# A hybrid decoder layer on one core: in blocks two to four the first two in-projection units multiply slice by slice, in two other PSUM banks

## The chip, the cores and the metric

The kernel runs on one core of a Trainium2 chip. The core has five engines that work side by side, each with its own instruction list, and they wait for one another through semaphores: TensorE (PE in the profile; its weight loads, PEld, overlap its matmuls), VectorE (DVE), ScalarE (ACT), GpSimd (POOL) and SyncE (SP), which here does nothing but issue DMA transfers. An engine takes its list strictly in order: an instruction that waits holds up everything behind it on that engine.

The metric is the device time of one execution in microseconds. Lower is better.

## The reference, cut to what matters

One layer over 2048 tokens of width 1024, in float32:

```python
h = rmsnorm(x, norm_mix_w) * (1 + sc1) + sh1
proj = h @ w_in                                   # 1024 x 3624
(hq, hf, hi, hg, sq, sk, sv, iq, ik, iw, cu) = split(proj)
o_a = hgrn2_mixer(hq, hf, hi, hg, ...)            # 4 heads, gated linear recurrence, chunkwise
o_b = dsa_mixer(sq, sk, sv, iq, ik, iw)           # indexer, top 256 keys per query, softmax
o_c = conv_module(cu, ...)                        # gate, causal depthwise conv (31 taps), LayerNorm, swish
x = x + g1 * (concat[o_a, o_b, o_c] @ w_out)
h = rmsnorm(x, norm_mlp_w) * (1 + sc2) + sh2
x = x + g2 * (relu(h @ W1) ** 2 @ W2)             # hidden width 4096
return rmsnorm(x, final_norm_w)
```

The part that matters here is `h @ w_in`, and the attention `dsa_mixer` and recurrence `hgrn2_mixer` that run beside it.

## The kernel before, in words

**Precision.** A float32 operand of a large matmul is split into a high and a low part (`ah`, `al` for activations; `whi`, `wlo`, or `wk` when both come back from a copy in HBM, for weights). One product is three matmuls: high by high, high weight by low activation, low weight by high activation.

**Blocks.** The 2048 tokens are done in four blocks of 512 (`b` is 0 to 3 in the code; the text says block one to four). For each block `in_block` does the norm, turns the activations, and then goes through 26 units of columns of `w_in` (`in_units`: 23 of 128 columns, and three of 256 that are done by L1280). A unit of 128 columns is 8 slices of 128 rows by three matmuls, so 24 matmuls of 128x512 into one PSUM bank (`mm_T`, L424). The first three units are the index keys with the index weights (`ev_index_k`) and the two index query units (`ev_iq`). The text calls them unit 0, unit 1 and unit 2; unit 3 is the first one of the recurrence.

**Turning the activations.** `to_act_steps` does one slice `k` of eight at a time: four PE transposes of 128x128 into a bank (L281), an ACT scale and shift into `tf` (L286), an ACT cast to the high part `ah` (L287) and the low part `al` by subtraction on DVE for slices 1, 4 and 6, on POOL for the others (L288). Every second slice the `mid` callback advances the recurrence of the block before.

**PSUM.** There are eight banks. The tag `mm` has two (transposes of slices and the units), `ax` two (the recurrence and small sums), `cx` one (convolution), `po` one (attention output) and `at` two. In this first half of the program the two `at` banks belong to the attention: its scores (L965), its turned probabilities (L987), the small turns L1011 and L1017, a count of the top-k search (L929) and the index scores (L808).

**Queues of side work.** After every unit a `step()` pumps generators: the recurrence (`fast`), the convolution, the modulation vectors, the index scores, the top-k search (DVE passes L917 with some small instructions, L918 to L926) and the attention (`at`). In blocks one to three, query tiles 0 to 5 of the attention are done; the others come later, beside the MLP. Per head the attention goes: scores on PE (L965), bias and maximum on DVE (L967, L976), exponential on ACT (L981), turn on PE (L987), copy and cast on ACT (L995, L996), low part on POOL (L997), product on PE (L999), and at the end of a head L1008 on ACT, L1009 on POOL, L1011 on PE, L1012 on ACT, L1013 on POOL.

**Who sets the order.** The program is recorded in the order of the code, and a scheduler then lays out each engine's list: it takes what it believes to be ready, earlier recorded work first, and gives a tile its bank only when the tile that had the bank before has been let go. So an instruction whose bank is still held is put behind others that were recorded later.

**Weights.** In blocks two to four the split weights of `w_in` come back from HBM (`wk<-wk_d`, issued on SP at L107) into slots used in turn: two units share the four `whi` and four `wlo` slots (of half a unit each), every third unit uses the two `wraw` slots. So unit 3 loads into the slots of unit 0, and can begin only when unit 0 has multiplied.

Of the kernel before, what the change touches and what calls it, by code (L numbers as in the profile page):

```python
# [43 lines left out]
KO, NPF = 2, 2  # L44
# [34 lines left out]
def trunk(ctx, tc, x, c, ada_w, ada_b, norm_mix_w, norm_mlp_w, w_in, hg_lb_logits,  # L79
# [22 lines left out]
    def nm(s):  # L102
        uid[0] += 1
        return f"{s}_{uid[0]}"
# [21 lines left out]
    def ps_at():  # L126
        return pp.tile([P, 512], F32, tag="at", bufs=2, name=nm("at"))

    def ps_xp(i):
        return {'0': ps_ax, '1': ps_mm, '2': ps_at, '3': ps_po}[XP[i]]()  # L130
# [79 lines left out]
    sh1 = cst.tile([P, NK], F32, name="sh1")  # L210
    a1 = cst.tile([P, NK], F32, name="a1")
# [63 lines left out]
    def to_act_steps(xh, acol, bcol, ah, al, mid=None):  # L275
        for k in range(NK):
            guard = tc.high_priority(offset=HA)
            guard.__enter__()
            pt = {'0': ps_ax, '1': ps_mm, '2': ps_at, '3': ps_po}[(TA2 if px['ax'] < 3 else TA)[k]]()
            for t in range(4):  # L280
                T.transpose(pt[:, t * P:(t + 1) * P], xh[t][:, k * P:(k + 1) * P], ident)  # L281
            hi = ap.tile([P, TB], F32R, tag="ah", bufs=8, name=nm("ah"))
            lo = ap.tile([P, TB], F32R, tag="al", bufs=8, name=nm("al"))
            tf = xp.tile([P, TB], F32, tag="tf", bufs=2, name=nm("tf"))
            ac, bc = acol[:, k:k + 1], bcol[:, k:k + 1]
            A.activation(tf, pt, AF.Identity, scale=ac, bias=bc)  # L286
            A.copy(hi, tf)  # L287
            (V if k in (1, 4, 6) else G).tensor_tensor(lo, tf, hi.bitcast(F32), OP.subtract)  # L288
            guard.__exit__(None, None, None)
            ah.append(hi)  # L290
            al.append(lo)
            if mid is not None and k % 2:
                mid()
            yield

    def to_act(xh, acol, bcol, mid=None):
        act = [], []
        for _ in to_act_steps(xh, acol, bcol, *act, mid):
            pass
        return act  # L300
# [22 lines left out]
    def by_k(tiles):  # L323
        return [t[:, k] for t in tiles for k in range(t.shape[1])]
# [73 lines left out]
    def next_w(pf=PF, ps=PS):  # L398
        top_up(pf, ps)
        w, sp = ready.pop(0)  # L400
        given.append((w, sp))
        return [by_k(t) for t in w]
# [12 lines left out]
    def mm_T(ps, w, act, k_outer=False, mid=None, k0=0, k1=NK):  # L415
        hi, lo = w
        ah, al = act
        prod = ((hi, ah), (hi, al), (lo, ah))
        if k_outer:
            order = [(k, p) for k in range(k0, k1) for p in prod]  # L420
        else:
            order = [(k, p) for p in prod for k in range(NK)]
        for n, (k, (ww, aa)) in enumerate(order):
            T.matmul(ps, ww[k], aa[k], start=(n == 0 and k0 == 0), stop=(n == len(order) - 1 and k1 == NK))  # L424
            if mid is not None and n == 11:
                mid()
# [603 lines left out]
    def pump(q, ns):  # L1030
        credit[q] += ns
        while queues[q] and credit[q] > 0:
            try:
                with tc.high_priority(offset=HF if q == "fast" else HC if q == "conv" else -LP):
                    r = next(queues[q][0])
                if r is None:
                    credit[q] = 0.0
                    break
                credit[q] -= r
            except StopIteration:  # L1040
                queues[q].pop(0)
        if not queues[q]:
            credit[q] = min(credit[q], 0.0)
# [21 lines left out]
    rates = {"fast": FAST, "conv": CR, "ada": 300.0, "idx": R1[0], "tk": R1[1], "at": R1[2]}  # L1065
# [30 lines left out]

    early = []

    def first_units(xts):
        act = [], []  # L1100
        steps = to_act_steps(xts, a1, sh1, *act)
        ws = []
        for k in range(NK // 2):
            next(steps)
        for u in range(KO):
            ws.append(next_w())
            early.append(ps_at())
            mm_T(early[u], ws[u], act, True, None, 0, NK // 2)
        ada_half(1, TB, a1, "nmix", far)
        ada_half(0, TB, sh1, None, far2)  # L1110
        for _ in steps:
            pass
        for u in range(KO):
            mm_T(early[u], ws[u], act, True, None, NK // 2, NK)
        return act

    def in_block(b, xts, nxt):
        act = first_units(xts) if b == 0 else to_act(xts, a1, sh1, lambda: pump("fast", rates["fast"]))
        for u, (pieces, ev, m) in enumerate(in_units):
            if ev is ev_cb:  # L1120
                drain("conv")
            if ev is ev_hf:
                drain("fast", 1)
            if u == PREP and b == NB - 1:
                yield "prep"
            if u == 1 and b == 0:
                late_consts()
            if b == 0 and u < len(early):
                ps = early[u]
            elif ev in (ev_hi, ev_sv):  # L1130
                ps = []
                halves = [[a[kh * 4:(kh + 1) * 4] for a in act] for kh in range(2)]
                ws = [next_w()]
                for tp_ in range(2):
                    ps.append(ps_xp(14 + tp_))
                    for kh in range(2):
                        if len(ws) < 2 and kh:
                            ws.append(next_w(1, 0))
                        n_part(ps[tp_], tp_, halves[kh], ws[kh], kh == 0, kh == 1)
                        if tp_ and kh:  # L1140
                            top_up()
                        half()
                    if tp_ == 0:
                        ev(b, m, ps[0], 0)
                        yield
            else:
                w = next_w()
                ps = ps_mm()
                mm_T(ps, w, act, u in (0, len(in_units) - 1), half)
            with tc.high_priority(offset=HE):  # L1150
                if ev is ev_index_k:
                    ev(b, ps)
                elif ev in (ev_hi, ev_sv):
                    ev(b, m, ps[1], 1)
                else:
                    ev(b, m, ps)
            keep_w()
            if ev is ev_ca and m == 1:
                queues["conv"].append(conv_gen(b))
            if ev is ev_hg:  # L1160
                queues["fast"].append(hgrn_gen(b, m, hg["q"], hg["k"], hg["f"], hg["v", m], hg["gate"]))
            yield
            if u == 2:
                yield "idx"
            if ev is ev_sv:
                yield "qkv"
            if u == NX:
                nxt()
# [498 lines left out]
```

## Time and profile before

| | |
|---|---|
| three runs, device us | 2903.92, 2909.93, 2911.09; median 2909.93 |
| the profiled execution | 2909.95, of which the span of the profile is 2908.2 |
| TensorE, busy and share of the span | 2781.8, 96% |
| VectorE | 1676.6, 58% |
| ScalarE | 1239.7, 43% |
| GpSimd | 1086.4, 37% |
| mean granted TensorE clock | 0.984 |
| the three stretches in which the activations of blocks two, three and four are turned (PE, from the first transpose to the first matmul of unit 0) | 243.9 to 261.3, 491.8 to 511.0, 741.4 to 755.1 |

A matmul's busy time in the profile includes a tail that overlaps the next one: thirteen of 128x512 in a row last 3.15 us, so they start 0.23 us apart, though each alone is shown with 0.39. For passes of 128x128 the figures are 0.27 shown and 0.11 apart. Sums of work below go by starts.

The idle time before an instruction is put down to what it waited for last. Engines other than TensorE are far from full over the whole span, but not everywhere: a stretch has to be looked at by itself.

### The profile page before, as it was taken

Reading aid. Unit: us, or ns where it says so; the run is one execution under the profiler, and the core shown is the slowest. Engines: PE = TensorE matmul, PEld = TensorE weight load, DVE = VectorE, ACT = ScalarE, POOL = GpSimd, SP = SyncE. Lnnn points to the kernel's source line nnn. Section 1 sums busy time; section 2 is a strip of 40 time slices with the busy share of each in tenths; the row PEclk is TensorE's granted clock in tenths of the full one; section 3 lists DMA queues with packets and bytes.
Section 4 is the critical chain, followed back from the end, with each engine's and each line's share of the span. In section 5 each row is a group of like instructions: output and inputs, shape, how many; then the busy total and the mean of one; then the engine's idle time right before and its main releaser. Section 6 shows DMA issues by size and latency. Waiting matters only on the chain.

```text
span 2908.2 us, 42801 instructions
## 1 busy us (share of the span) xinstructions
PE 2781.8 (96%) x14116; PEld 2306.0 (79%) x14116; DVE 1676.6 (58%) x3514; ACT 1239.7 (43%) x2630; POOL 1086.4 (37%) x1051
## 2 busy tenths in 40 slices
PE   5999998999999989999999999999999998999997
PEld 4888887888788777888777888887788887777776
DVE  6695697777465437656757637477662221254455
ACT  4436444533311244555556444354643332343323
POOL 7444111212100445666665222234422223345444
PEclk9999999999999989999999999999999999999999
DMA  9987676667655668898888776677867666686676
GB/s 292 291 268 243 215 234 190 218 209 245 202 183 180 221 218 255 272 291 284 292 266 295 231 221 216 202 243 258 289 211 237 200 226 197 217 284 209 224 235 206
DMA packets 428074, 688.61 MB, mean 237 GB/s; under 512 B 43383, under 2 KB 171452, under 8 KB 427836
## 3 DMA queue, kind: packets, MB, share of 16 engines
q1 hardware_dynamic: 427680, 685.67, 72.9%
q8 instruction: 113, 1.85, 0.3%
q14 instruction: 125, 1.02, 0.1%
q10 hardware_dynamic: 156, 0.07, 0.0%
HBM read 532.74 MB, written 152.84 MB: 236 GB/s over the span
## 4 chain that ended last, share of the span: by engine, by line
PE 41%; DMA 5%; DVE 4%; POOL 1%; issue 1%; ACT 0%; SPq 0%; POOLq 0%; DVEq 0%; ACTq 0%
PE mm L1304 10%; PE mm L424 9%; PE ax L424 7%; PE ax L1304 6%; PE mm L1464 4%; PE at L965 1%; PE po L999 1%; DMA wk<-wk_d 1%; PE at L987 1%; PE ix L808 1%; DMA tr<-in_mlp_w_dram 1%; PE at L1304 1%; DVE s L815 1%; DVE cum L917 1%; POOL wk L376 1%
## 5 line engine op out<-in xcount | busy, mean ns | idle before, releaser
L424 PE MATMUL mm<-ah,wk 128*128 128x512 f32 x1920 | 513.2, 399 | 4.1 <-DVE slo L537 1.7
L424 PEld LDWEIGHTS mm<-ah,wk 128*128 128x128 f32 x1920 | 355.7, 190 | 78.5 <-DVE slo L537 2.0
L318 POOL TENSOR_TENSOR wlo<-wraw,whi 128x512 fp32r<-128x512 f32 x210 | 285.8, 1380 | 245.2 <-ACT whi L317 133.6
L997 POOL TENSOR_TENSOR pT<-L,pT 128x512 fp32r<-128x512 f32 (+3 forms) x160 | 193.3, 1210 | 374.9 <-ACT pT L996 194.3
L815 DVE SCALAR_TENSOR_TENSOR s<-r,iw_s,s 128x512 f32<-128x512 f32 (+3 forms) x266 | 239.2, 899 | 104.2 <-ACT r L810 95.6
L424 PE MATMUL mm<-al,wk 128*128 128x512 f32 x960 | 262.4, 395 | 0.0
L967 DVE CUSTOM_DVE_ANT_0 L<-at,bias 128x512 f32<-128x512 f32 (+3 forms) x152 | 93.6, 619 | 206.0 <-PE at L965 156.7
L424 PEld LDWEIGHTS mm<-al,wk 128*128 128x128 f32 x960 | 178.3, 189 | 36.0
L1304 PE MATMUL mm<-wk,hh 128*128 128x512 f32 x640 | 197.8, 398 | 1.5 <-ACT tf L286 1.1
L810 ACT ACTIVATE r<-ix 128x512 f32<-128x512 f32 (+3 forms) x256 | 133.2, 554 | 151.6 <-PE ix L808 113.0
L317 ACT CAST whi<-wraw 128x512 fp32r<-128x512 f32 x210 | 122.1, 620 | 162.6 <-DMA wraw<-in_mlp_w_dram 47.9
L273 POOL TENSOR_TENSOR hl<-hr,hh 128x512 fp32r<-128x512 f32 x96 | 129.6, 1351 | 161.3 <-ACT hh L265 159.5
L424 PE MATMUL ax<-ah,wk 128*128 128x512 f32 x720 | 187.1, 393 | 1.4 <-DMA wk<-wk_d 1.4
L588 DVE SCALAR_TENSOR_TENSOR cx<-hc,cvc,cx 128x512 f32<-128x512 f32 x232 | 173.7, 749 | 2.0
L917 DVE TENSOR_SCALAR_CACHE_REDUCE cum<-s,ssm 128x384 bf16<-128x384 f32 (+13 forms) x112 | 165.3, 1476 | 7.3 <-POOL s L819 5.2
L995 ACT COPY L<-at 128x512 f32<-128x512 f32 (+3 forms) x160 | 82.8, 522 | 180.6 <-PE at L987 179.0
L424 PEld LDWEIGHTS ax<-ah,wk 128*128 128x128 f32 x720 | 134.2, 188 | 31.2 <-ACT hc L1438 1.8
L1464 PE MATMUL mm<-wk,hc 128*128 128x512 f32 x588 | 148.4, 397 | 4.9 <-DVE acc L1472 4.9
L981 ACT ACTIVATE L<-L,nmx 128x512 f32<-128x512 f32 (+3 forms) x160 | 103.8, 650 | 97.9 <-DVE nmx L976 97.7
L1304 PEld LDWEIGHTS mm<-wk,hh 128*128 128x128 f32 x640 | 117.9, 188 | 27.4 <-ACT tf L286 1.6
L1464 PEld LDWEIGHTS mm<-wk,hc 128*128 128x128 f32 x588 | 109.4, 188 | 35.3 <-DVE acc L1472 8.7
L1304 PE MATMUL ax<-wk,hh 128*128 128x512 f32 x384 | 123.8, 400 | 1.7 <-DMA wk<-wk_d 1.4
(364 smaller groups left out, 6096.4 us busy)
## 6 DMA issues: line engine op xcount, KB each, us to landing
wk<-wk_d SPq DMA_DIRECT2D x776, 256.0 KB
wk<-wk_d SPq DMA_DIRECT2D x196, 512.0 KB
wk_d<-whi SPq DMA_DIRECT2D x210, 256.0 KB
wk_d<-wlo SPq DMA_DIRECT2D x210, 256.0 KB
wraw<-in_mlp_w_dram SPq DMA_DIRECT2D x68, 512.0 KB
kc<-sk_d SPq DMA_DIRECT2D x112, 256.0 KB
vc<-v_d SPq DMA_DIRECT2D x112, 256.0 KB
adw<-in_ada_w_dram SPq DMA_DIRECT2D x128, 128.0 KB
```

The costliest lines, as they stand in the source:

```text
L273: e.tensor_tensor(lo[:, i:j], src[:, i:j], hi[:, i:j].bitcast(F32), OP.subtract)
L317: A.copy(hi, src)
L318: G.tensor_tensor(lo, src, hi.bitcast(F32), OP.subtract)
L424: T.matmul(ps, ww[k], aa[k], start=(n == 0 and k0 == 0), stop=(n == len(order) - 1 and k1 == NK))
L588: V.scalar_tensor_tensor(acc if w < TAPS - 1 else total, hc[:, w:w + TB], cvc[:, m, w:w + 1], acc, op0=OP.mult, op1=OP.add)
L810: A.activation(r[:, :w], ps[:, :w], AF.Relu, scale=32.0 ** -0.5)
L815: V.scalar_tensor_tensor(s[:, c0:c0 + w], r[:, :w], iw, s[:, c0:c0 + w], op0=OP.mult, op1=OP.add)
L917: V.tensor_scalar(dump, s, t, -AIM - i * STEP, op0=OP.is_ge, op1=OP.add, accum_out=d)
L981: A.activation(lt[:, :w], lt[:, :w], AF.Exp, bias=nmx, accum_out=sm[:, cb:cb + 1])
L997: G.tensor_tensor(pT[:, :nt, 1], lv, pT[:, :nt, 0].bitcast(F32), OP.subtract)
L1304: T.matmul(ps, aa[f][:, tok * P:(tok + 1) * P], ww[i], start=(first and n == 0), stop=(last and n == 5))
L1464: T.matmul(bank[t], aa[:, k, t * P:(t + 1) * P], ww[k], start=(i in (0, 2, 4) and n == 0), stop=(n == 5), skip_group_check=True)
```

## The change

In block one nothing changes. In blocks two to four `to_act` is replaced by the new `paced_units`: it takes the weights of units 0 and 1, asks for the two `at` banks, and then, after each slice of the activations, multiplies that slice for both units (three matmuls each). Units 0 and 1 are then evicted from the `at` banks where they used to be evicted from `mm` banks. The number of matmuls, transposes, evictions and transfers is the same.

```diff
+    def paced_units(xts):
+        act = [], []
+        ws = [next_w(), next_w(1, 0)]
+        early[:] = [ps_at() for _ in range(KO)]
+        for k, _ in enumerate(to_act_steps(xts, a1, sh1, *act, lambda: pump("fast", rates["fast"]))):
+            for u in range(KO):
+                mm_T(early[u], ws[u], act, True, None, k, k + 1)
+        return act
+
...
     def in_block(b, xts, nxt):
-        act = first_units(xts) if b == 0 else to_act(xts, a1, sh1, lambda: pump("fast", rates["fast"]))
+        act = (paced_units if b else first_units)(xts)
...
-            if b == 0 and u < len(early):
+            if u < len(early):
                 ps = early[u]
```

`KO` is 2, `NK` is 8. How the lists of the engines move is shown at three places. A name's number only tells tiles apart.

**Block two, TensorE, at the end of the transposes.** Before, unit 0 (`mm_3205`) follows the last transposes at once:

```order
L281 MATMUL mm_3181<-ident,xt_2350 128x128
L1011 MATMUL at_3007<-ident,ot_3004 128x128
L987 MATMUL at_3018<-ident,L_2945 128x128 x3
L424 MATMUL mm_3205<-ah_3087,wk_2854 128x512
L424 MATMUL mm_3205<-al_3088,wk_2854 128x512
```

Now what follows is unit 2 (`mm_3593`, in an `mm` bank), and units 0 and 1 (`at_3086`, `at_3087`) stand 48 rows later, behind the attention's last query tile of that time:

```order
L281 MATMUL mm_3229<-ident,xt_2350 128x128
L1011 MATMUL at_3007<-ident,ot_3004 128x128
L987 MATMUL at_3018<-ident,L_2945 128x128 x3
L424 MATMUL mm_3593<-ah_3093,wk_3082 128x512
...
L987 MATMUL at_3067<-ident,L_3058 128x128
L965 MATMUL at_3077<-kc_3075,qs_3046 128x128 x2
L723 MATMUL ax_2691<-v_2160,kt_2657 128x128 x4
L733 MATMUL ax_2724<-v_2160,at_2304 128x128
L735 MATMUL ax_2724<-S_st_196,q_2046 128x128
L733 MATMUL ax_2724<-v_2160,at_2304 128x128
L424 MATMUL at_3086<-ah_3093,wk_2854 128x512
```

Between the two pieces stand the 24 matmuls of unit 2 and small work of attention, recurrence and convolution; no other unit.

**Block three, TensorE and VectorE, where the attention lets go of the banks.** Before, the last scores of the query tile at hand (`at_6384`) stood far inside the units, among the matmuls of a wide one:

```order
L1280 MATMUL mm_6962<-wk_6846,ah_6451 128x256
L965 MATMUL at_6384<-kc_6382,qs_6099 128x128 x2
L1280 MATMUL mm_6962<-wk_6846,ah_6462 128x256
```

Now, of the units, only unit 2 stands ahead of them, and unit 0 (`at_6397`) begins behind them:

```order
L735 MATMUL ax_6050<-sa_6024,q_5260 128x128
L965 MATMUL at_6384<-kc_6382,qs_6099 128x128 x2
L999 MATMUL po_6346<-pT_6356,vc_6349 128x256 x4
L424 MATMUL at_6397<-ah_6404,wk_6165 128x512
L424 MATMUL at_6397<-al_6405,wk_6165 128x512
```

On VectorE the instruction that frees the bank `at_6384` needs (the L967 that reads `at_6367`) has moved ahead of all evictions of units 0 and 1, but still stands behind five passes of the top-k search, the last of which is here:

```order
L917 TENSOR_SCALAR cum_5857,ssm_5865<-s_4379,ssm_5865 128x768
L918 TENSOR_SCALAR ssm_5865<-ssm_5865 128x1
L922 TENSOR_SCALAR ssm_5865<-ssm_5865 128x1
...
L925 TENSOR_SCALAR ssm_5865<-ssm_5865 128x1
L967 ISA L_6370,mx_6364<-at_6367,bias_4399 128x512
```

From the L967 of the query tile's first scores (`at_6108`) to the one of `at_6384` there are 87 rows, and 92 instructions with the reads that follow each L917.

**Block four, TensorE.** Here no attention holds the banks. Before, the units came behind the last transposes:

```order
L281 MATMUL mm_9119<-ident,xt_8514 128x128
L695 MATMUL ax_8569<-q_8236,k_8170 128x64 x4
L424 MATMUL mm_9147<-ah_9025,wk_8918 128x512
L424 MATMUL mm_9147<-al_9026,wk_8918 128x512
```

Now they stand among the transposes, from the third slice on:

```order
L281 MATMUL mm_9062<-ident,xt_8501 128x128
L424 MATMUL at_9022<-ah_9029,wk_8912 128x512
L424 MATMUL at_9023<-ah_9029,wk_8963 128x512
L695 MATMUL ax_8611<-q_8225,k_8164 128x64 x4
L281 MATMUL mm_9079<-ident,xt_8474 128x128
...
L424 MATMUL at_9022<-al_9030,wk_8912 128x512
L424 MATMUL at_9022<-ah_9029,wk_8914 128x512
L424 MATMUL at_9023<-al_9030,wk_8963 128x512
L424 MATMUL at_9023<-ah_9029,wk_8964 128x512
```

On SP the loads of unit 3's weights, which before stood ahead of the next attention loads, now stand behind them, since unit 0 lets go of its slots later. From the MLP on, the lists of all engines are nearly the same as before.

## The prediction

> **What bounds the kernel now.** I read the page first, then the waits of TensorE, then the stretches around the three places that change.
>
> ```profile
> span 2908.2 us, 42801 instructions
> PE 2781.8 (96%) x14116; PEld 2306.0 (79%) x14116; DVE 1676.6 (58%) x3514; ACT 1239.7 (43%) x2630; POOL 1086.4 (37%) x1051
> ```
>
> TensorE is busy for 2782 of 2908 us. All that any reordering can win is in the other 126 us, and whatever idle time is put into TensorE's list is paid nearly in full. The waits of TensorE, as us in total, times, longest:
>
> ```profile
> PE mm L281 <- ACT tf L286: 13.4, 12, 2.5
> ...
> PE at L1304 <- DMA wk<-wk_d: 7.4, 3, 5.6
> ```
>
> The first row is the wait that the change aims at, but over all eight turnings of activations (block one, and four in the MLP, have it too). The stretches, with busy time, number of instructions, and granted clock:
>
> ```profile
> core 0: us, PE busy (x) PEld busy (x) DVE busy (x) ACT busy (x) POOL busy (x), PEclk, DMA share, GB/s
> 243.90:261.30 17.40, 13.49 (x92) 11.96 (x90) 11.70 (x29) 14.07 (x28) 8.53 (x10) 0.90 0.35 113
> 261.30:275.00 13.70, 13.70 (x80) 11.01 (x79) 9.16 (x14) 9.81 (x21) 9.43 (x14) 1.00 0.72 255
> ...
> 491.80:511.00 19.20, 13.59 (x68) 10.68 (x66) 17.90 (x45) 13.04 (x32) 6.82 (x7) 0.75 0.32 91
> 511.00:515.00 4.00, 3.97 (x9) 3.14 (x10) 4.00 (x13) 2.02 (x3) 1.23 (x1) 0.50 0.97 383
> 515.00:545.00 30.00, 29.60 (x169) 24.75 (x168) 28.37 (x92) 16.36 (x33) 8.49 (x14) 1.00 0.67 218
> 741.40:755.10 13.70, 10.38 (x78) 8.76 (x76) 8.19 (x22) 12.23 (x28) 6.23 (x6) 1.00 0.42 141
> ```
>
> While slices are turned TensorE idles 3.9, 5.6 and 3.3 us in blocks two, three and four, and runs below full clock in two of them (block three pays another 4 x 0.5 = 2 us right behind). If every slice were multiplied at once, about 13 us of idle time and some 5 us of clock would be there to win. Behind the stretch TensorE is full: 13.70 of 13.70.
>
> **The change, part by part.** Counts stay: 144 matmuls move from `mm` to `at` banks, 24 per unit, two units, three blocks. Their evictions are the same instructions on another bank, so I cost both at nothing; each stands on ACT and DVE, which have room over the span. What decides is when the two `at` banks come free, and the lists show that this differs by block.
>
> *Block two.* The transposes stay as they are, unit 2 comes next, and unit 0 waits for the last attention tile. How long this chain takes is read from the same instructions in the trace of before:
>
> ```profile
> 268.37 0.51 PE L999 MATMUL po<-pT,vc 128*128 128x256 f32 x3
> ...
> 286.02 0.27 PE L717 MATMUL ax<-ident,k 128*128 128x128 f32 x1
> 286.13 0.28 PE L609 MATMUL ax<-ones,cu 128*128 128x1 f32 x2
> ...
> 292.09 1.05 PE L723 MATMUL ax<-v,kt 128*128 128x128 f32 x8
> ...
> 300.66 1.12 PE L1280 MATMUL mm<-wk,ah 128*128 128x256 f32 x8
> ...
> 532.61 3.15 PE L424 MATMUL mm<-ah,wk 128*128 128x512 f32 x13
> ```
>
> (So passes start 0.11 us apart at 128 columns, (1.12 - 0.28) / 7 = 0.12 at 256, (3.15 - 0.39) / 12 = 0.23 at 512.)
>
> ```profile
> 270.90 0.35 ACT L1008 COPY ot<-po 128x256 f32<-128x256 f32 x1
> ...
> 275.24 0.37 ACT L1012 ACTIVATE ot<-at,rd 128x128 f32<-128x128 f32 x1
> ...
> 282.59 0.41 ACT L981 ACTIVATE L<-L,nmx 128x128 f32<-128x128 f32 x1
> ...
> 287.19 0.59 ACT L719 COPY kt<-ax 128x512 f32<-128x512 f32 x1 [4.09 <-PE ax L717]
> ```
>
> ```profile
> 272.91 0.92 POOL L1009 TENSOR_TENSOR ot<-ot 128x128 f32<-128x128 f32 x1
> ```
>
> L1009 ends at 273.8, and nothing ahead of it changes. From there, without matmuls in between: L1011 and L1012 to 274.4, L965 and its L967 and maximum to 275.6, L981 to 276.2, the copy L719 behind it to 277, L723 to 278.2, and three small passes: unit 0 can begin at about 278.5 instead of 261.3. In these 17.2 us TensorE has 24 x 0.23 = 5.5 us of unit 2 and about 7 us of small work (the passes named in the rows above with L695, L597, L703 and L609), so 12.5: **4.7 us idle**. Bounds: 3 if the small work is dearer (a pass shows 0.27 where its successor starts 0.11 later), 8 if ACT's list, which now has L1019, L981 and L719 close together, loses as much again. I take 5.
>
> *Block three.* Here three heads of a query tile with 640 keys stand ahead of unit 0, and VectorE is the engine that paces them: it was 17.90 of 19.20 and 28.37 of 30.00 us busy in the rows above. Its list begins at the same point:
>
> ```profile
> 516.11 0.67 DVE L967 CUSTOM_DVE_ANT_0 L<-at,bias 128x512 f32<-128x512 f32 x1
> ...
> 567.10 0.28 DVE L967 CUSTOM_DVE_ANT_0 L<-at,bias 128x128 f32<-128x128 f32 x1
> ```
>
> The second row is the last scores' L967, 51 us later in the old order. In the new list it is 92 instructions after the first. What these cost is seen from the groups between 516 and 545 us (busy, mean ns):
>
> ```profile
> L917 DVE TENSOR_SCALAR_CACHE_REDUCE cum<-s,ssm 128x768 bf16<-128x768 f32 x7 | 7.0, 1006 | 0.1
> L435 DVE TENSOR_SCALAR xt<-xt,rs 128x1024 f32<-128x1024 f32 x4 | 3.0, 744 | 0.9 <-POOL rs L255 0.9
> L697 DVE COPY_PREDICATED at<-lmask,ax 128x256 f32<-128x256 uint8 x4 | 2.0, 504 | 0.0
> L926 DVE TENSOR_SCALAR ssm<-ssm 128x1 f32<-128x1 f32 x7 | 1.9, 267 | 0.1
> L660 DVE TENSOR_TENSOR q<-q,fb 128x256 f32<-128x256 f32 x4 | 1.7, 427 | 0.0
> L924 DVE TENSOR_SCALAR ssm<-ssm 128x1 f32<-128x1 f32 x6 | 1.6, 273 | 0.2
> ```
>
> Five passes of the search (1.0 each, and six small ones of 0.16 to 0.27), four L435, four L697, six pairs of L660 and L661, two L599 and the attention's own come to 31 us by the column of means. Tails overlap: 92 instructions took 30 us here with seven L917 against five. So 26 to 29 us, and I take 27. The banks are then free at 516 + 27 = 543. TensorE's own work from 511 until then: unit 2, 5.5 us, and small work that I get by taking away. In the old order the same small work was done between 511 and 572:
>
> ```profile
> L424 PE MATMUL mm<-ah,wk 128*128 128x512 f32 x80 | 22.8, 413 | 1.1 <-ACT tf L286 1.1
> L424 PE MATMUL mm<-al,wk 128*128 128x512 f32 x40 | 12.0, 412 | 0.0
> L1280 PE MATMUL mm<-wk,ah 128*128 128x256 f32 x64 | 10.7, 290 | 0.0
> L1280 PE MATMUL mm<-wk,al 128*128 128x256 f32 x32 | 5.6, 289 | 0.0
> ```
>
> 120 x 0.23 = 27.5 and 96 x 0.12 = 11.5 are units, 2 is clock, 1.5 idle; 18.5 of the 61 us is left, of which some 3.5 come after the banks are free. So 15 + 5.5 = 20.5 us of work in 32: 11.5 idle. The 2 us at half clock now fall into that idle time (a gain of 2), but the idle time itself can lower the clock again at the start of unit 0 (0 to 2, I take 1). **Block three: 10.5 us lost**, between 6 (VectorE at 24 us, since the evictions of units 0 and 1 are out of its way) and 15 (its waits on ACT and PE added).
>
> The Trainium skill (TensorE: Matmul & The Clock Gate, Part 1) has the clock at half after about 3.4 us of idle and full again after about 3.4 us of work, which agrees with 0.50 in the 4 us behind the turning of block three. By that rule both stalls would be followed by a slow start, as an estimate 1.7 us each; the sum would be higher by about 2.
>
> *Block four.* No attention is in the way, and units 0 and 1 do as the change says:
>
> ```profile
> 747.25 0.66 PE L281 MATMUL mm<-ident,xt 128*128 128x128 f32 x4 [1.68 <-ACT tf L286]
> ```
>
> This is the largest of the gaps that sum to 3.3 us. ACT, 12.23 of 13.70 busy, still paces the slices, but 48 matmuls of 0.23 (11 us) now lie beside them, and only the gaps before the third slice stay open. **3 us won**, 2 to 4.
>
> *Weights.* In blocks two and three unit 2 is gone when units 0 and 1 end, and unit 3 must wait for the second half of its weights, which can start only when unit 0 is through (before, units 1 and 2 covered this load). On SP the loads are issued behind attention loads that are themselves done by then. Waits for `wk` above are 7.4 us in three, so 2.5 each; about 1.5 us of small passes cover part. I take 1 us in each of the two blocks, 0 to 2.5. In block four unit 2 stands behind units 0 and 1 again and covers the load: nothing.
>
> *Given back.* Attention and recurrence have run ahead by then. Later in the blocks TensorE had waits of its own:
>
> ```profile
> 420.00:470.00 50.00, 46.72 (x307) 42.85 (x306) 36.95 (x111) 18.80 (x55) 10.37 (x16) 0.93 0.71 217
> ...
> 580.00:620.00 40.00, 38.57 (x207) 31.87 (x206) 24.82 (x61) 10.09 (x20) 1.96 (x5) 0.96 0.70 215
> ```
>
> With 3.3 and 1.4 us in these two stretches, 0 to 4 us could come back; most belong to the next heads of the recurrence, which start no earlier. I take 1.5.
>
> **Sum.** 5 + 10.5 - 3 + 2 - 1.5 = 13 us more. Against the profiled execution's 2909.95 (span 2908.2 and 1.75 around it) this is 2923. The median of the three runs is 2909.93, so the sum stands for it too.
>
> **Rivals.**
>
> *The stalls are half as long.* If the attention's chain runs faster once TensorE is free for it, the banks of block three come free near 536 and those of block two near 275: 2.5 + (4.5 - 2 + 1) + 2 - 3 - 1.5 = 3.5, time 2913. For it: no engine but VectorE is full there. Against it: VectorE is, and its order is fixed.
>
> *Faster.* The early attention and search pay back all the later waits, and block four wins its 3: 2.5 + 4 - 4 - 4 and the clock's 2 + 1, time about 2905. It needs the stall of block three under 5 us, that is VectorE through 92 instructions in 20 us, 0.22 each, where it took 0.33. The Trainium skill (Perfetto Trace Analysis, Matmul Optimizations) asks for all eight PSUM banks to be used, which speaks for giving idle `at` banks to the units; the lists show that in blocks two and three they are not idle.
>
> *Slower still.* The chain in block three waits on ACT as well: its list has a table load, four L259 and the exponentials ahead of the first copy that frees a bank, and I have these at 5.5 us:
>
> ```profile
> 515.63 1.06 ACT L259 ACTIVATE xdump<-xt 128x1024 bf16<-128x1024 f32 x1 [1.94 <-DVE al L288]
> ...
> 519.93 1.28 ACT L981 ACT_TABLE_LOAD   x1
> ```
>
> If each of the three heads takes 3.5 us longer and unit 3 finds no weights after it (2.5 twice), the loss is 13 + 10.5 + 3 = 26.5, time 2936. From about 12 us of idle in block three on this decides.
>
> **How the numbers follow.** Forecast 0.62, half stalls 0.20, faster 0.06, slower still 0.12. With every bound at its end at once the forecast goes from 2911 (3 + 6 - 4 + 0 - 4 = 1) to 2936 (8 + 15 - 2 + 5 - 0 = 26). Its own half of that would be narrower, but the half stalls and most of the slower rival lie inside these ends too, so I keep them as the range; outside lie the faster rival and the far part of the slower one. A measurement of this kernel can tell 0.3% (8.7 us) from no change. Slower by more: nearly all of the forecast, the slower rival, and a little of the half stalls, 0.77. Within: 0.18. Faster by more than 0.3% needs nearly the whole gain, 0.05.
>
> **What would show it.** In the changed profile: TensorE goes from the transposes of block two and three to unit 2 and then shows gaps before `at` matmuls of L424, put down to ACT or VectorE steps of the attention; about 17 us from the last transposes to unit 0 in block two and 32 in block three; VectorE close to full in the second; no gap of over a microsecond while block four's slices are turned; a short wait for `wk` before unit 3. The prediction is wrong if units 0 and 1 of block three begin within 22 us of the transposes, or if the idle time of the rest of the first half falls by as much as the stalls add.

## The result, and the profile after

The changed kernel takes 2935.14 us (median of four, 2931.07 to 2938.26) beside 2910.51 for the kernel before: ratio 1.0094, 95% interval 1.0075 to 1.0112. A second set of six, taken later as a control, gave 2931.70 beside 2912.15: 1.0065, 1.0045 to 1.0084. So the change costs about 20 to 25 us by the medians, 19 to 27 by the ratios. The forecast was 2923, 13 us more, with a range up to 2936. The direction holds and the median lies just inside the range (the first ratio, taken to 2909.95, gives 2937, just outside); the size is one and a half to two times the forecast.

The head of the page of the changed kernel, profiled in an execution of 2935.74 us:

```profile
span 2933.6 us, 42795 instructions
PE 2790.3 (95%) x14116; PEld 2313.6 (79%) x14116; DVE 1678.9 (57%) x3514; ACT 1238.2 (42%) x2628; POOL 1077.8 (37%) x1051
```

TensorE has the same 14116 matmuls and is busy 8.5 us longer, in a span that is 25.4 us longer. Its waits, as us in total, times, longest:

```profile
PE mm L281 <- ACT tf L286: 9.5, 9, 2.3
...
PE mm L281 <- DVE gate L656: 6.8, 2, 4.1
...
PE mm L424 <- DMA wk<-wk_d: 1.7, 1, 1.7
```

The wait that the change aims at fell from 13.4 to 9.5. The second row is a wait that no part of the prediction had; the third is the wait for unit 3's weights, once, where I had it twice at 1 us.

The stretches of the changed kernel, in the columns of the stretches before (length, then busy time of the engines, granted clock behind POOL): block two's turning and the stall from unit 2 to unit 0, the same for block three, and block four's turning.

```profile
243.80:263.50 19.70, 16.11 (x91) 14.61 (x90) 12.52 (x30) 14.29 (x28) 9.05 (x10) 0.72 0.33 100
263.50:283.20 19.70, 17.01 (x96) 14.19 (x96) 10.87 (x27) 12.06 (x29) 10.62 (x17) 0.76 0.53 177
501.30:521.10 19.80, 11.56 (x63) 8.99 (x61) 18.44 (x47) 12.27 (x29) 6.57 (x7) 0.76 0.42 138
521.10:555.30 34.20, 28.26 (x155) 23.36 (x155) 27.98 (x92) 19.55 (x49) 15.03 (x21) 0.79 0.34 114
769.10:792.00 22.90, 18.78 (x104) 15.89 (x103) 9.44 (x21) 10.61 (x16) 6.45 (x5) 0.93 0.33 103
```

In each, idle is length less PE's busy time, and the clock's loss is busy time times one minus the granted clock. Both together are the time that a full TensorE at full clock would not have needed:

| us lost (idle + clock) | before | after |
|---|---|---|
| block two, turning | 3.9 + 1.3 | 3.6 + 4.5 |
| block two, unit 2 to unit 0 | 0 | 2.7 + 4.1 |
| block three, turning (before, with the 4 us behind it) | 5.6 + 5.4 | 8.2 + 2.8 |
| block three, unit 2 to unit 0 (before: 515 to 545) | 0.4 + 0 | 5.9 + 5.9 |
| block four, turning | 3.3 + 0 | 4.1 + 1.3 |
| sum | 20 | 43 |

These rows hold 23 of the 25 us. From the MLP on the two kernels differ by 2: its first transposes come at 1021.0 before and 1044.4 after. That small difference hides something that no part of the prediction had: from there on TensorE idles 67.8 us where it idled 62.7, and in this execution 4.5 us less of half clock give most of it back. In the control it idles 67.3 there, and that part takes 5.8 us longer than before. The cause is open. The halves, idle 11 and clock 12, are those of one execution; over ten executions of the changed kernel the mean granted clock was 0.9806, over 82 of the kernel before 0.9846, and 0.004 of some 2920 us is again 12 of the 22 us between their means (roughly, since this mean counts idle time too).

In block two, TensorE's rows of the changed kernel from the last attention turn to unit 0 (start, us; in brackets the idle time ahead and what ended it):

```profile
273.92 0.33 PE L1011 MATMUL at<-ident,ot 128*128 128x128 f32 x1 [0.83 <-POOL ot L1009]
...
276.36 0.48 PE L1017 MATMUL at<-ident,ob 128*128 128x128 f32 x1 [1.03 <-POOL ob L1013]
...
277.67 0.45 PE L717 MATMUL ax<-ident,k 128*128 128x128 f32 x1 [0.84 <-DVE k L661]
...
280.40 2.08 PE L723 MATMUL ax<-v,kt 128*128 128x128 f32 x8
...
283.24 0.48 PE L424 MATMUL at<-ah,wk 128*128 128x512 f32 x1
```

Two of the gaps stand ahead of the attention's turns, where the prediction had them, one ahead of the recurrence's L717. What it had not: L723 takes 2.08 us where it took 1.05, at half clock. Unit 0 begins at 283.2, 4.7 us later than forecast (1.3 in the control, at 279.8).

In block three:

```profile
521.10 3.76 PE L424 MATMUL mm<-ah,wk 128*128 128x512 f32 x8
...
540.14 0.33 PE L1011 MATMUL at<-ident,ot 128*128 128x128 f32 x1 [1.00 <-POOL ot L1009]
...
546.57 0.58 PE L999 MATMUL po<-pT,vc 128*128 128x256 f32 x1 [1.03 <-POOL pT L997]
...
555.32 0.39 PE L424 MATMUL at<-ah,wk 128*128 128x512 f32 x1
```

From unit 2 to unit 0 are 34.2 us, against 32 forecast. VectorE's first and last L967 of this stretch, and TensorE in the last 8.7 us ahead of unit 0:

```profile
520.73 0.68 DVE L967 CUSTOM_DVE_ANT_0 L<-at,bias 128x512 f32<-128x512 f32 x1
...
555.10 0.29 DVE L967 CUSTOM_DVE_ANT_0 L<-at,bias 128x128 f32<-128x128 f32 x1 [0.25 <-PE at L965]
```

```profile
546.60:555.30 8.70, 8.70 (x51) 8.57 (x52) 5.09 (x22) 3.67 (x12) 3.23 (x5) 0.65 0.22 53
```

VectorE's list takes 34.4 us where the prediction had 27. Up to 535 us it waits 0.6 us in all; behind that it waits 5.3 us, of which 4.9 are for TensorE. And TensorE is not waiting at the end: it works without a gap up to unit 0, at a mean clock of 0.65.

### The profile page after: what moved, and what is told of

Read it like the earlier page. It is cut to its first block, busy times and chain, and to the rows that moved or that the text cites. A ratio compares the mean times of both kernels' runs of the same rounds, so it can differ in the third digit from the quotient of the medians.

```text
span 2933.6 us, 42795 instructions
## 1 busy us (share of the span) xinstructions
PE 2790.3 (95%) x14116; PEld 2313.6 (79%) x14116; DVE 1678.9 (57%) x3514; ACT 1238.2 (42%) x2628; POOL 1077.8 (37%) x1051
## 4 chain that ended last, share of the span: by engine, by line
PE 40%; DVE 4%; DMA 4%; POOL 2%; issue 1%; ACT 1%; SPq 0%; POOLq 0%; DVEq 0%; ACTq 0%
PE mm L1313 10%; PE mm L424 8%; PE ax L424 7%; PE ax L1313 5%; PE mm L1473 4%; PE po L999 1%; PE at L965 1%; PE at L987 1%; PE at L1313 1%; DMA wk<-wk_d 1%; DVE cum L917 1%; PE ix L808 1%; DVE s L815 1%; DMA tr<-in_mlp_w_dram 1%; DMA wraw<-in_mlp_w_dram 1%
## 5 line engine op out<-in xcount | busy, mean ns | idle before, releaser
L424 PE MATMUL mm<-ah,wk 128*128 128x512 f32 x1824 | 484.3, 398 | 2.8 <-DMA wk<-wk_d 1.7
L424 PEld LDWEIGHTS mm<-ah,wk 128*128 128x128 f32 x1824 | 338.1, 190 | 72.7 <-DMA wk<-wk_d 1.9
L424 PE MATMUL mm<-al,wk 128*128 128x512 f32 x912 | 251.1, 397 | 0.0
L967 DVE CUSTOM_DVE_ANT_0 L<-at,bias 128x512 f32<-128x512 f32 (+3 forms) x152 | 93.7, 620 | 198.9 <-PE at L965 147.8
L424 PEld LDWEIGHTS mm<-al,wk 128*128 128x128 f32 x912 | 169.6, 190 | 34.8 <-issue 0.9
L917 DVE TENSOR_SCALAR_CACHE_REDUCE cum<-s,ssm 128x384 bf16<-128x384 f32 (+13 forms) x112 | 165.4, 1476 | 8.0 <-POOL s L819 6.0
```

Source lines behind the costliest of these rows:

```text
L917: V.tensor_scalar(dump, s, t, -AIM - i * STEP, op0=OP.is_ge, op1=OP.add, accum_out=d)
```

## The experiments

Times are medians; each ratio is to the kernel before, run on the same chip in the same session (there 2911.2 to 2912.2).

**Each block alone.** The condition on the block is narrowed, here to block two, in the other two kernels with `(2,)` and `(3,)`; the blocks left out are as before:

```diff
-        act = (paced_units if b else first_units)(xts)
+        paced = b in (1,)
+        act = (first_units(xts) if b == 0 else paced_units(xts) if paced else
+               to_act(xts, a1, sh1, lambda: pump("fast", rates["fast"])))
...
-            if u < len(early):
+            if u < len(early) and (b == 0 or paced):
```

> The change in block two alone; blocks three and four as before. Bank theory (units 0 and 1 wait until the attention lets go of the two at banks, and the idle time brings the clock down): block two is 9.7 us longer in the changed profile, of which some 5 us is a longer stretch at half clock during the turning itself, where the lists do not differ yet. So +5 to +10 us, 2915 to 2920. Rival, order and weights (two units interleaved by slice, unit 2 ahead of them and unit 3 without weights cost the same wherever it is done): a third of 24.6 in each block, +8, 2918. The pair with the next two tells.

> The change in block three alone. Bank theory: the largest loss, since three attention heads stand ahead of unit 0 there: +13 to +18, 2923 to 2928; unit 0 begins some 35 us behind the last transposes. Rival, order and weights: +8, 2918.

> The change in block four alone, where no attention holds the banks. Bank theory: a small gain or nothing, -4 to 0, 2906 to 2910; the gaps between the transposes fill. Rival, order and weights: +8, 2918.

| changed | us | ratio, 95% interval | us more, from the ratio |
|---|---|---|---|
| block two | 2924.55 | 1.0049 (1.0034 to 1.0064) | +14 |
| block three | 2921.22 | 1.0038 (1.0023 to 1.0052) | +11 |
| block four | 2910.51 | 0.9997 (0.9985 to 1.0008) | -1 |

The three sum to 24, so the parts add up. Both stalls are real; block two costs more than expected (5 to 10) and block three less (13 to 18). Block four shows no gain, though its interval, -4.4 to +2.3 us, does not exclude the 3 us forecast. That it costs nothing speaks against the rival of +8 in each block. Block four alone, its turning and the rest of the block:

```profile
739.50:763.00 23.50, 23.50 (x143) 20.11 (x142) 11.85 (x29) 14.02 (x30) 7.61 (x7) 1.00 0.53 182
...
800.00:1022.00 222.00, 210.48 (x1193) 178.50 (x1191) 123.57 (x235) 50.10 (x126) 44.14 (x42) 0.98 0.60 192
```

and the rest of the block in the kernel before:

```profile
800.00:1021.00 221.00, 212.82 (x1236) 181.52 (x1235) 123.08 (x235) 50.06 (x127) 42.79 (x40) 1.00 0.61 198
```

The turning is without any idle time: the 3.3 us are won there, as forecast. From 800 us on TensorE idles 11.5 us where it idled 8.2, so in this execution 3.3 us come back. Its waits for steps of the recurrence there (L717, L723, L703, L748, L670) are 7.0 us, against 3.8 before.

**The other way round.** The transposes go into the `at` banks and units 0 and 1 into `mm`:

```diff
-            pt = {'0': ps_ax, '1': ps_mm, '2': ps_at, '3': ps_po}[(TA2 if px['ax'] < 3 else TA)[k]]()
+            pt = (bank or {'0': ps_ax, '1': ps_mm, '2': ps_at, '3': ps_po}[(TA2 if px['ax'] < 3 else TA)[k]])()
...
-        early[:] = [ps_at() for _ in range(KO)]
-        for k, _ in enumerate(to_act_steps(xts, a1, sh1, *act, lambda: pump("fast", rates["fast"]))):
+        early[:] = [ps_mm() for _ in range(KO)]
+        for k, _ in enumerate(to_act_steps(xts, a1, sh1, *act, lambda: pump("fast", rates["fast"]), ps_at)):
```

> The change in all three blocks with the banks exchanged: the transposes of the slices go through the two at banks, a few us each, and units 0 and 1 multiply slice by slice in the two mm banks. Bank theory: the attention can slip in between the transposes, no unit waits for it, both stalls are gone and the gaps between the transposes are filled: -5 to -15, 2895 to 2905. Rival, order and weights: the units are interleaved as in the change, so the loss stays, 2925 to 2935.

Measured 2941.01, ratio 1.0100 (1.0080 to 1.0119): a miss by more than 30 us. TensorE's rows of block two:

```profile
264.48 0.69 PE L965 MATMUL at<-kc,qs 128*128 128x128 f32 x2 [0.59 <-ACT ot L1012]
...
268.19 1.97 PE L281 MATMUL at<-ident,xt 128*128 128x128 f32 x8
```

The first transposes, at 243.9 before, now stand at 268.2, behind the same attention. Whoever asks for the `at` banks waits for it, and the transposes were the worse choice, for everything hangs on them.

**The banks kept free.** The change is left whole, but the attention, index scoring and search are not offered for interleaving from unit 21 of block one, and from unit 12 of block two, to unit 2 of the next block; beside it the same hold in the kernel before, without the change.

```diff
-            pump(q, rates[q])
+            if not (hold[0] and q in ("idx", "tk", "at")):
+                pump(q, rates[q])
...
+            hold[0] = u >= (21 if b == 0 else 12) and b < 2 or b in (1, 2) and u < 2
```

> The change in all three blocks, and beside it the attention, the index scoring and the search passes are not offered for interleaving between the last third of a block (unit 21 on in block one, unit 12 on in block two) and unit 2 of the next block, so that nothing holds the two `at` banks when units 0 and 1 want them: in the engine order their passes now stand between the slices in blocks two, three and four. Nothing is left out; the held work comes later in the block. Theory A (what costs is the time in which the attention keeps the banks, about 12 us of idle and what the clock loses behind it): both stalls vanish, units 0 and 1 fill the idle of the transposes in blocks two and three as they do in block four, and the time is 2895 to 2915, not over that of before. Rival B (the slice-by-slice passes cost by themselves, by more PSUM evictions, weight reads or the order of operands): 2925 to 2940, as with the whole change. Rival C (the held attention only meets the projections later): 2915 to 2930, with gaps at the `at` tiles later in blocks two and three.

> The kernel before, with the same hold as in the held kernel (attention, index scoring and search not offered for interleaving from unit 21 of block one and unit 12 of block two to unit 2 of the next block), and without the change. It tells what of the held kernel's 0.9989 is the hold's and what the change's. Theory A (with the banks free the change itself is worth what it fills): the hold alone is 2908 to 2918, so the change on top of it gains 0 to 10 us. Rival B (the hold alone gains, and the change costs on top of it): 2895 to 2905.

Change and hold: 2908.08, ratio 0.9989 (0.9978 to 1.0001). Hold alone: 2915.07, 1.0006 (0.9993 to 1.0018). The 20 to 25 us are gone, so the slice-by-slice passes cost nothing by themselves; what costs is the wait for the banks. Blocks two and three of the held kernel, in their turning:

```profile
242.10:257.40 15.30, 15.30 (x95) 12.98 (x94) 8.26 (x18) 11.22 (x20) 5.22 (x4) 1.00 0.28 91
476.30:495.00 18.70, 15.94 (x86) 12.98 (x84) 15.93 (x52) 11.48 (x26) 5.63 (x6) 0.91 0.32 102
```

Block two's turning has no idle time left, block three's 2.8 us. Yet the whole is barely under the kernel before: block four, with the held attention in it, takes 289.7 us from transposes to transposes against 279.7.

**What keeps the banks in block three.** Only the search passes are held, from unit 20 of block two to unit 4 of block three (the same edit with `("tk",)` and `b == 1 and u >= 20 or b == 2 and u < 4`).

> The whole change, and only the search passes (VectorE, L917) are not offered between unit 20 of block two and unit 4 of block three; the attention itself is left where it is. In the engine order units 0 and 1 of block three then stand between the slices from the third on, and block two's turning is as in the whole change. Theory A (in block three VectorE's share in the attention's chain keeps the banks, and block two loses by itself): block three's stall goes, block two's stays, and the time is 2918 to 2928, 7 to 17 us under the whole change's 2935. Rival B (VectorE's passes are not what keeps the banks): the stall before the first pass of unit 0 in block three stays over 25 us from the start of unit 2, and the time 2930 to 2940. Rival C (the search is only late): the next blocks lose what block three wins, 2928 to 2938.

Measured 2922.25, ratio 1.0044 (1.0028 to 1.0059), as with the change in block two alone. Block three's turning, with units 0 and 1 among the slices from the third on:

```profile
496.10:515.40 19.30, 15.93 (x85) 13.17 (x84) 17.83 (x45) 11.58 (x28) 7.24 (x7) 0.82 0.32 105
```

With the search held, that stall goes (3.4 us idle and 2.9 of clock are lost in the turning, where turning and stall lost 11.0 + 11.8). This does not single VectorE out, though. The attention needs the search's result (`bias`, read by L967), so it moves too: its first scores (L965) of block three come at 527.4 us, behind units 0 and 1, where they came at 504.1 in the changed kernel. And part of the gain is paid back in block four, which takes 287.3 us against 275.3 in the changed kernel.

**The gaps filled.** The changed kernel with useless repetitions of attention matmuls, where TensorE waits in the stalls:

```diff
+            for i in range(3 * (seen["kc"] in (4, 19, 21))):
+                T.matmul(ps[:, (i % 3 + 1) * P:(i % 3 + 2) * P], qs[:, 0, h, :], kc[:, :w], start=True, stop=True, skip_group_check=True)
...
+                for i in range(6 * (seen["po"] in (16, 17, 18))):
+                    T.matmul(po[:, 2 * P:], vc[:, 0, :], pT[:, 0], start=True, stop=True, skip_group_check=True)
```

> The whole change, and in the stalls of blocks two and three some of the attention's matmuls are repeated into columns of their own PSUM bank that nobody reads: three more of 128 columns after one score in block two; in block three three more after one score, and six more of 256 columns behind each of three groups of the weighted sums. About 4 us of useless TensorE work stand where TensorE waits about 1 us each time; the rest of the order is nearly unchanged. Nothing of the result is left out. Theory A (the dearer part of the two stalls is the clock that falls in them, about 9 us in block three's stretch and 4 in block two's): with the gaps filled the granted clock stays at 1.00 from about 533 to 552 us, the small work there takes half as long, and the time falls to 2925 to 2932 though work is added. Rival B (only the idle time counts): the same 2935 as with the whole change where every useless matmul fits its gap, or up to 4 us more, and the clock's rows do not matter.

> The changed kernel itself, unaltered, as the control of the kernel with filled gaps, and for a mean of span and granted clock over more executions than four. Theory (the loss is half idle and half clock): over all runs the span times one minus the granted clock is 53 to 59 us against 44 to 46 before, and the rest of the span 2874 to 2880 against 2864; time 2931 to 2939, that is 5 to 13 above the kernel with filled gaps. Rival (the filled gaps gained nothing, and the control's chip differs): 2923 to 2930.

Filled: 2925.95, ratio 1.0061 (1.0041 to 1.0081). The control: 2931.70, 1.0065 (1.0045 to 1.0084). The medians are 5.8 us apart, but from two chips, and the intervals of the ratios overlap almost wholly: the two can't be told apart, and the expectation of a clock at 1.00 failed. Unit 2 to unit 0 of block three, in the filled kernel and then in the control:

```profile
510.00:544.10 34.10, 29.84 (x181) 23.89 (x182) 29.29 (x100) 20.34 (x52) 14.81 (x22) 0.85 0.38 131
```

```profile
514.80:549.00 34.20, 28.24 (x155) 23.38 (x155) 27.95 (x92) 19.57 (x49) 15.02 (x21) 0.79 0.34 111
```

With the useless work or without, at 0.85 or 0.79, the stretch lasts 34.1 or 34.2 us. This does not show what the clock costs there, for the filling did not keep it up: behind unit 2 the clock is at 0.50 for 10.2 us in both kernels, from 524.3 to 534.5 in the filled one, from 529.3 to 532.7 and 539.5 to 546.3 in the control. The trace of the changed kernel speaks for a cost, since its half-clock work (0.50 from 545.9 to 552.7) stands in the piece without a gap that leads up to unit 0; how much shorter the stretch would be at full clock stays open. (Over all executions the mean clock was 0.983 filled and 0.980 in the control; whether that is worth anything, six executions each don't settle.)

**Why block four gained nothing in the changed kernel.** TensorE and then VectorE there:

```profile
773.79 1.26 PE L281 MATMUL mm<-ident,xt 128*128 128x128 f32 x8 [4.12 <-DVE gate L656]
```

```profile
770.13 0.48 DVE L199 SCALAR_TENSOR_TENSOR adacc<-adw,cact,adacc 128x256 f32<-128x256 f32 x1 [0.85 <-DMA adw<-in_ada_w_dram]
772.65 0.49 DVE L199 SCALAR_TENSOR_TENSOR adacc<-adw,cact,adacc 128x256 f32<-128x256 f32 x1 [2.03 <-DMA adw<-in_ada_w_dram]
773.05 0.69 DVE L656 TENSOR_TENSOR gate<-mm,gate 128x512 f32<-128x512 f32 x1
```

The second transposes wait for an `mm` bank that L656 lets go, and L656 stands on VectorE behind two sums of the modulation vectors, which wait 2.9 us for their weights. So those sums were held at that place:

```diff
+            if not (hold[0] and q == "ada"):
...
+            hold[0] = b == 2 and u >= 22 or b == 3 and u < 2
```

> The whole change, and the modulation vectors' side work (the sums L199 on VectorE, each of which needs a weight transfer) is not offered between unit 22 of block three and unit 2 of block four. On VectorE the eviction L656, which frees the `mm` bank that block four's second transposes wait for, then has no L199 ahead of it. Theory (in the changed kernel block four's gain is lost to this queue: TensorE waited 4.12 us for L656, which stood behind an L199 that waited 2.03 us for its transfer): no wait for L656 at that place, block four's turning at under 2 us of idle, and the time 2925 to 2931, that is 3 to 6 under the changed kernel's 2932 to 2935. Rival (the vectors are made up later, or the gain of the turning comes back in the block as it did with the change in block four alone): the gap goes, and the time stays at 2930 to 2937.

Measured 2924.06, ratio 1.0050 (1.0033 to 1.0067). Block four's turning:

```profile
759.80:775.50 15.70, 13.87 (x91) 11.85 (x91) 8.35 (x19) 10.22 (x16) 5.36 (x5) 1.00 0.26 88
```

L656 has no L199 ahead of it, and 1.8 us are lost where 5.4 were. The block from transposes to transposes takes 272.4 us against 275.3 (274.2 in the control). That accounts for 2 to 3 of the 8 to 11 us by which the kernel is under the changed one; the rest is not placed.

Block four's length alone misleads here, since it was 279.6 us before: in the changed kernel it is shorter, though more is lost in it, because work has moved ahead (TensorE is busy for 264.2 us of it, against 268.1, and for 247.0 of block three, against 239.3). What counts is the time lost. With the sums held TensorE idles 8.8 us in the whole of block four, at full clock; before, it idled 11.5, also at full clock. In this one execution the forecast's 3 us are there.

**Towards a version that beats both.** The change in blocks two and four alone, with the hold only ahead of block two:

> The change in blocks two and four alone, with the hold only ahead of block two (from unit 21 of block one to unit 2 of block two), where little attention is pending. Nothing is left out. Theory A: block two's banks are free, its slices fill the transposes as in the held kernel (whose block two took 234.1 us against 247.9 before), block three is as before, block four gains its 1 to 3: 2900 to 2910 in all. Rival B (what block two wins comes back when the held attention is made up in block two or three): 2910 to 2920.

2915.14, ratio 1.0011 (0.9997 to 1.0025). Block two took 235.7 us, 12 less than before, but block three 255.6, 6 more, and block four 282.3, 3 more: rival B. Then the held kernel with the hold ending as soon as the units of the next block begin (`u < 0` for `u < 2` in its last line):

> The held kernel with a shorter hold: the attention, index scoring and search are offered again from unit 0 of the next block on instead of unit 2, so that less of it is made up later. Theory (the deferred attention is what the held kernel pays in block four, 289.7 us against 279.7): block four's interval 280 to 287, and 2902 to 2908 in all, under the kernel before by a little. Rival (the attention comes back into the banks before units 0 and 1 are evicted, and the stall with it): 2912 to 2925.

2898.50 (2894.15 to 2905.84), ratio 0.9953 (0.9936 to 0.9970): 13 us under the kernel before, the fastest of all. The turnings of blocks two, three and four:

```profile
242.10:257.40 15.30, 15.30 (x95) 13.02 (x94) 8.27 (x18) 11.25 (x20) 5.22 (x4) 1.00 0.30 96
479.90:500.00 20.10, 15.38 (x96) 12.52 (x95) 13.57 (x34) 12.99 (x29) 8.44 (x8) 1.00 0.40 121
720.70:735.20 14.50, 14.50 (x97) 12.89 (x96) 8.35 (x22) 12.08 (x28) 6.04 (x6) 1.00 0.32 107
```

4.7 us are lost in the three, where the kernel before lost 19.5. The time came out 3.5 us under the range expected, and not where it was expected: block four takes 287.6 us, hardly less than in the held kernel, and block three 240.8 against 247.8. The short hold without the change was not run, so how much of the 13 us is the change's stays open.

## Why the prediction was right in direction and short in size

Where the time is lost, and what holds the banks, was right; the sum was not, 13 us against 25 in the profiled execution. The step that failed is the credits, 6.5 us that were set against the losses. The largest is block four's: 3 us won in the forecast, 2 us lost in the run, because TensorE waited 4.1 us for an `mm` bank there (3.7 in the control). Besides, block two's stall was costed 2 us too small.

*Where the stalls are, and why.* Right for the banks: units 0 and 1 wait for the attention in blocks two and three, and the hold removes both stalls. That VectorE's list sets the pace in block three holds in the trace only up to about 535 us; behind that VectorE waits for TensorE as well. No run separates the search from the attention that needs it.

*Block three, 11.5 us idle in the stall.* Right in size, in part by luck. The stretch lost 11.9 us, and the control 11.9 as well, but only half of that is idle; the other half is TensorE at half clock. And the 32 us of the stretch were built from two times that were off in opposite directions: VectorE's list took 34.4 us instead of 27, and it began 0.4 us ahead of unit 2 instead of 5 us behind it. I had the list at VectorE's own pace, with no wait for TensorE. VectorE was also less full than I had it, 27.98 of 34.2 us.

*Block three, 2 us of half clock that fall into the idle time.* Did not come. What stands behind the turning is not idle time but unit 2, and it runs at half clock: 0.51 from 521.1 to 525.5. This is part of the stall's 5.9 us of clock. In the turning itself 8.2 us are idle where 5.6 were. The 1 us for a slow start of unit 0 did not come either: from 555.3 to 569.0 TensorE is full at 1.00.

*Block two, 5 us.* Short. 6.8 us were lost between unit 2 and unit 0, in 19.7 us (19.2 in the control) where I had 17.2. I costed the chain at full clock, and it runs partly through TensorE: after two gaps of about 1 us the clock was at 0.50 from 276 to 283, and the passes that the chain needs (L717, L723) took twice their time. By the Trainium skill (TensorE: Matmul & The Clock Gate, Part 1), idle of about one window of 3.4 us halves the clock; the sum by it was 15, still short. The trace does not agree with what I made of it: no single gap here was that long, the half clock stood inside the stalls, and behind both of them unit 0 began at 1.00. In the kernel before, where I had the rule in agreement, the longest wait in block three's turning was 1.8 us.

*Block four, 3 us won.* This is the step that failed by most: +2 instead of -3 in the turning. With the change in block four alone the turning wins its 3.3 us, and that much idle time comes back later in the block. In the changed kernel the turning meets a VectorE queue that waits for a transfer; with that queue's sums held, the block as a whole idles 2.7 us less than before. I had looked at who holds the new banks, not at who is late to free the old ones.

*Weights, 2 us.* Nearly right: 1.7 us once, in block three, where I had 1 us in each of two blocks.

*Given back, 1.5 us.* Not settled. Outside the turnings and stalls, and without the wait for weights, blocks two and three idle as long in the profiled execution as before (0.4 us more), but 3 us less in the control.

So the losses, 5 + 11.5 + 1 + 2 = 19.5, were nearly right in sum; against 2909.95 they give 2929.5. The three credits, 2 + 3 + 1.5 = 6.5, failed in this execution, and block two was 2 short. In the profiled execution another 3 us are the clock in block two's turning, whose lists the change does not touch; the control had 15.80 us there, with the clock at 1.00:

```profile
245.20:261.00 15.80, 12.43 (x93) 10.71 (x92) 11.27 (x29) 14.57 (x29) 9.07 (x10) 1.00 0.37 122
```

*The rivals.* "Slower still" came closest in time, but not by its mechanism: VectorE's list in block three took 7 us longer than forecast, yet it waited for TensorE (4.9 us) and hardly for ACT (0.4), the stretch became only 2 us longer, and unit 3 waited for its weights once. "Faster" had its condition wrong only in this kernel: with the banks free, the turnings of the kernel with the short hold lose 14.8 us less, of the 13 us of idle and 5 of clock that the first part of the prediction called there to win, and that kernel is 13 us faster.

## What to carry to other kernels

Before work is moved into a resource that seems spare, list who holds it at that moment and which engine sets when they let go; then move the holder, not only the work. The same change cost 20 to 25 us with the holder in place and was part of a gain of 13 with it held back for half a block. Book losses at full and credits only where it is shown what uses the time won: here block four's credit went to a queue that waited for a transfer, and with that block changed alone no gain was left to measure.

## What the runs showed of the hardware

Half clock needs no long gap. In block three's stall of the changed kernel:

```profile
527.00:531.00 4.00, 4.00 (x26) 3.45 (x25) 3.37 (x11) 3.97 (x8) 3.37 (x7) 1.00 0.49 169
531.00:535.00 4.00, 1.78 (x12) 1.24 (x11) 4.00 (x9) 0.61 (x3) 2.63 (x4) 1.00 0.53 181
535.00:539.00 4.00, 3.63 (x11) 2.45 (x11) 2.87 (x10) 1.20 (x4) 0.63 (x1) 0.58 0.26 66
```

TensorE was busy for 1.78 of 4 us, in pieces between gaps of at most 1 us, and ran at half clock for most of the next 4. In block two the same: busy for 1.71 of the 3.4 us from 272.8 on, at full clock, and then 0.50 for 6.8 us. Nor is busy time alone enough to bring the clock back at once: in the same kernel TensorE worked without a gap from 257.1 to 266.0, at 0.50 throughout. And the clock is not the same from one execution to the next: the control is the same kernel, and its turning of block two ran at 1.00 throughout, against 0.72 in the other profile, 3.4 us lost against 8.1. The kernel before spread over 2901 to 2922 us in 82 executions.
